# A hybrid decoder layer: four heads' values and gMLP's second half as a fourth pair of block products

## Chip, cores and metric

The kernel runs on one core of one Trainium2 chip. The metric is the device time of one execution in microseconds. A core has five engines that each work through their own list of instructions in order: TensorE (PE in the profile, with PEld for its weight loads), VectorE (DVE), ScalarE (ACT), GpSimd (POOL) and SyncE (SP), which issues most transfers. 16 DMA engines carry data between HBM and the on-chip memory SBUF; PE writes its sums into PSUM, eight banks of 128x512 float32, four of which are called acc and four dn here.

## What is computed

One layer with parallel groups of heads on 1024 tokens of width 2048, and a final RMSNorm (cut):

```
h = rmsnorm(x, ln_g)
proj = h @ w_in                       # 2048 -> 7184 columns
g_u, g_v, g_z, d_q, d_k, d_v, d_z, d_a, d_b, c_q, c_z = split(proj)
out_a = gmlp_spatial_gating(g_u, g_v, ...) * silu(g_z)      # 512 wide; layernorm(gelu(g_v)) goes in
q, k, v = split(causal_conv_silu(concat(d_q, d_k, d_v)))    # 8 heads of 128
o = gated_delta_rule(l2norm(q), l2norm(k), v, g(d_a), sigmoid(d_b))
out_b = rmsnorm(o, dn_norm_g) * silu(d_z)                   # 1024 wide
out_c = softmax(c_q mk^T) mv * silu(c_z)                    # 4 heads, 256 memory tokens
out = rmsnorm(x + concat(out_a, out_b, out_c) @ w_out, final_g)
```

The delta rule runs over the tokens in chunks: a step needs the state that the step before it left.

## The kernel before

*Numbers.* A product in float32 is made of three matmuls in a faster 32-bit format (fp32r). Each operand is split into hi, a rounded copy (ScalarE), and lo, the rest (VectorE subtracts), by split_to (416), and triple (453) adds hi hi, hi lo and lo hi in a PSUM bank. So each element that goes through PE costs a copy on ScalarE and a subtraction on VectorE first.

*Order.* No engine's order is written by hand. Every operation is recorded with a rank (a priority), and Plan (63) sorts them with prices of its own for each operation; line 274 then emits all of them, which is why nearly every row of the profile names L274. Rank 1 goes first, 9 last. together() keeps matmuls side by side, behind(op) holds back what is recorded until op is done.

*Stages.* Tokens are handled in two halves of 512 (HT), in row tiles of 128. The normalised input stands in SBUF as ahi/alo, transposed, first of half 0, then of half 1.
1. Memory's keys and values, small preparations, and the normalisation of half 0.
2. half(0) and half(1) (811): each first projects gMLP's v, tokens in rows, over 16 blocks of K into four banks (the loop at the start of half), applies gelu and a layer norm and stores it; then the decays; then for the four pairs of heads front (q and k by proj, convolution, the block matrix), values (1113: v by proj, convolution) and back (1120). proj (459) makes 128 columns for 512 tokens: 16 blocks of K, 48 matmuls of 128x512. In half(0) w_piece (433) also stores each lo part of a weight in DRAM (low), and half(1) loads it from there.
3. inverse (985) inverts the 32x32 diagonal blocks of a pair of heads on VectorE, 31 steps of two instructions over 32 partitions; levels (1014) joins them to 128x128 by small matmuls; scan_step (1061) is the recurrence, eight steps for a pair of heads and half: k times state (PE), r (VectorE), u times r (PE), ww (ScalarE), then q times state and kd times ww (PE), the new state (VectorE), ai times ww (PE), a copy (ScalarE).
4. project_pair (1274) for three pairs of 512 columns each: d_z; c_z and c_q; gMLP's z and u. Here the product of two halves of tokens, two halves of K and two halves of columns is made from seven block products in place of eight (Winograd's form of Strassen's scheme): seven (1187) makes product m from a left block (of h, or a sum of blocks, s_d) and a right block (of the weights, or a sum), each 8 blocks of K into four banks. The sums of products are made in SBUF: take1 to take7 add a bank to the tiles y.
5. out_pair (1498), twice: the same scheme for w_out on the mixed outputs, then x is added, the sums of squares taken and close (1467) scales each row tile by its root and by final_g, and sends it out, four transfers of 256 KB for each row tile and half. Products come in the order 1, 7, 6, 4, 5, 3, 2. In the second out_pair half 1 is closed at product 5 and half 0 at product 2, the last one, whose last chunks are held back so that its row tiles end one after another (last=True).

left_sums and right_sums (726, 738) make the blocks' sums, as jobs spread over stage 2; third_sum and mix_done (1327, 1364) make those of the mixed outputs on GpSimd. rights_made (1241) makes right sums of weights in SBUF; products 1 to 3 use blocks as they are, 4 to 7 sums or differences.

Of the kernel before, what the change touches and what calls it, by code (L numbers as in the profile page):

```python
# [9 lines left out]
F32 = mybir.dt.float32  # L10
# [10 lines left out]
NQ = 4  # L21
# [256 lines left out]
def kernel(  # L278
# [50 lines left out]
    class Slots:  # L329


        def __init__(self, tag, n, shape):
            self.tag, self.n, self.shape, self.i, self.made = tag, n, list(shape), 0, [None] * n

        def __call__(self, dt=F32, slot=None):
            k = self.i % self.n if slot is None else slot
# [64 lines left out]


    ident, ones, utri, mneg = (C([P, P], n) for n in ("ident", "ones", "utri", "mneg"))
# [23 lines left out]
    def split_piece(raw, eng):  # L427
        hi, lo = whi(), wlo()
        with rank(2):
            split_to(hi, lo, raw, eng)  # L430
        return hi, lo

    def w_piece(src, keep=None, first=True):

        if first:
            hi, lo = split_piece(raw_piece(src), V)
            if keep is not None:
                Q.dma_start(keep, lo.bitcast(F32))
            return hi, lo
        raw, hi, lo = raw_piece(src), whi(), wlo()  # L440
        with rank(4):
            Q.dma_start(lo.bitcast(F32), keep)
        with rank(2):
            S.copy(hi, raw)
        return hi, lo
# [3 lines left out]
    def mm(a, lhs, rhs, start, stop):  # L449
        with rank(9):  # L450
            return PE.matmul(a, lhs, rhs, start=start, stop=stop)

    def triple(a, l, r, start, stop):

        mm(a, l[0], r[0], start, False)
        mm(a, l[0], r[1], False, False)
        return mm(a, l[1], r[0], False, stop)

    def proj(w, c0, rhs, keep, first):

        a = main_bank()
        for kp in range(KT // KP):
            hi, lo = w_piece(
                w[kp * KP * P : (kp + 1) * KP * P, c0 : c0 + P].rearrange("(k p) c -> p k c", p=P), keep[kp], first
            )
            hi, lo = tok(hi), tok(lo)
            for kk in range(KP):
                k = kp * KP + kk
                triple(a, (hi[:, kk], lo[:, kk]), rhs(k), k == 0, k == KT - 1)
                if kk == 0:  # L470
                    marks.append(R.ops[-3])
        return a
# [38 lines left out]
    mrow = C([16, P], "mrow")  # L511
# [41 lines left out]
    def prep(tt, put, bank):  # L553
# [3 lines left out]
        for q in range(NQ):  # L557
            V.scalar_tensor_tensor(xq[q], xq[q], r, gb[q], op0=ALU.mult, op1=ALU.mult)
            tp = bank()
            for k in range(4):  # L560
                PE.transpose(tp[:, k * P : (k + 1) * P], xq[q][:, k * P : (k + 1) * P], ident)
            put(q, tok(tp))

# [72 lines left out]
    for h in range(NX):  # L636
# [8 lines left out]
    G.memset(mneg, 0.0)  # L645
    G.affine_select(out=mneg, in_=mneg, compare_op=ALU.is_ge, fill=NEG, base=0,
                    pattern=[[1, P]], channel_multiplier=-1)
    rows = C([96, P], "rows")
    Q.dma_start(rows, conv_w.rearrange("k (c p) -> (k c) p", p=P))
    rows2 = C([9, P], "rows2")  # L650
    Q.dma_start(rows2[0:4], gmlp_ln_g[0].rearrange("(c p) -> c p", p=P))
    Q.dma_start(rows2[4:8], gmlp_ln_b[0].rearrange("(c p) -> c p", p=P))
    Q.dma_start(rows2[8:9], dn_norm_g)
# [8 lines left out]
    PE.transpose(pt[:, 0:96], rows, ident[0:96, 0:96])  # L662
    cw = C([P, 96], "cw")
    V.tensor_scalar(cw, pt[:, 0:96], 0.5, None, op0=ALU.mult)
    pt = dnr()
    PE.transpose(pt[:, 0:9], rows2, ident[0:9, 0:9])
    col2 = C([P, 9], "col2")
    V.tensor_scalar(col2[:, 0:8], pt[:, 0:8], 0.25, None, op0=ALU.mult)
    V.tensor_scalar(col2[:, 8:9], pt[:, 8:9], 0.5, None, op0=ALU.mult)
# [41 lines left out]
    mix_d = [[DT([P, HT], f"mixd{h}_{k}") for k in range(KT)] for h in range(2)]  # L711
    hT_d = DT([KT, P, HT], "hTd")
# [3 lines left out]
    h0_d = DT([KT, P, HT], "h0d")  # L716
    o_d = [[DT([P, HT], f"od{h}_{i}") for i in range(NH)] for h in range(2)]
    v_d = [[DT([P, NT, P], f"vd{h}_{g}") for g in range(NG)] for h in range(2)]
# [4 lines left out]
    t_d = [[DT([P, HT], f"td{j}_{i}") for i in range(4)] for j in range(NH)]  # L723
    left, right = slice(0, HT), slice(HT, 2 * HT)

    def left_sums(src, dst):
        a, b, c, d = (ring["zg"]() for _ in range(4))
        with rank(6):
            for t, x_ in zip((a, b, c, d), src):
                Q.dma_start(t, x_)  # L730
            V.tensor_tensor(out=d, in0=c, in1=d, op=ALU.add)
            V.tensor_tensor(out=c, in0=a, in1=c, op=ALU.subtract)
            V.tensor_tensor(out=a, in0=d, in1=a, op=ALU.subtract)
            V.tensor_tensor(out=b, in0=b, in1=a, op=ALU.subtract)
            for t, x_ in zip((d, a, c, b), dst):
                Q.dma_start(x_, t)

    def right_sums(src, dst):
        a, b, c, d = (ring["zg"]() for _ in range(4))
        with rank(6):  # L740
            for t, x_ in zip((a, b, c, d), src):
                Q.dma_start(t, x_)
# [4 lines left out]
            for t, x_ in zip((a, d, b, c), dst):  # L747
                Q.dma_start(x_, t)

    def blk(w, k, c0):  # L750
        return w[k * P : (k + 1) * P, c0 : c0 + HT]

    def keep_h(q):
        for k in range(4 * q, 4 * q + 4):
            t = ring["zg"]()
            with rank(6):
                G.tensor_tensor(out=tok(t), in0=ahi[k], in1=alo[k], op=ALU.add)
                Q.dma_start(h0_d[k], t)

    def right_job(j):  # L760
        (c1, c2), k1, k2 = pairs[0], j, NH + j
        right_sums((blk(w_in, k1, c1), blk(w_in, k1, c2), blk(w_in, k2, c1), blk(w_in, k2, c2)), t_d[j])

    jobs = [lambda q=q: keep_h(q) for q in range(NQ)]
    jobs += [lambda j=j: right_job(j) for j in range(NH)]
    jobs += [lambda j=j: left_sums((h0_d[j], h0_d[NH + j], hT_d[j], hT_d[NH + j]), s_d[0][j]) for j in range(NH)]

    def next_job(mark=None):
        if jobs:
            with behind(mark or marks[-1]):  # L770
                jobs.pop(0)()

    def put1(tt):
        def put(q, tp):
            t = ring["tn"]()
            S.copy(t, tp.rearrange("p t c -> p (t c)"))
            Q.dma_start(hT_d[4 * q : 4 * q + 4, :, tt * P : (tt + 1) * P].rearrange("k p n -> p k n"), tok(t))

        return put

    def refill(src, k, eng):

        raw = wraw()
        Q.dma_start(raw, src[k])
        split_to(ahi[k], alo[k], tok(raw), eng)

    def wide_banks():
        i, j = turn["acc"] % 2, turn["tp"] % 2
        return [acc[1 - i], acc[3 - j], acc[i], acc[2 + j]]

    def tanh_gate(a, o):

        t = ring["tn"]()
# [4 lines left out]
    def gelu2(a, o):  # L798

        t = ring["tn"]()  # L800
# [8 lines left out]
    low_d = {}  # L809

    def half(hf):
        def project(c0):
            if hf == 0:
                low_d[c0] = [DT([P, HT], f"low{c0}_{kp}") for kp in range(KT // KP)]
            return proj(w_in, c0, ahl, low_d[c0], hf == 0)

        def to_tokens(src):
            tp = tpb()
            for tt in range(NT):
                PE.transpose(tp[:, tt * P : (tt + 1) * P], src[:, tt * P : (tt + 1) * P], ident)  # L820
            return tok(tp)


        vk = [ring[tag]() for tag in ("ai", "ai", "kd", "kd")]
        aa = wide_banks()
        for k in range(KT):
            if hf == 1:
                refill(hT_d, k, V)
            w = w_piece(w_in[k * P : (k + 1) * P, C_V : C_V + GW])
            for tt in (2, 3, 0, 1) if k == KT - 1 else range(NT):  # L830
                vmark = triple(aa[tt], (ahi[k][:, tt], alo[k][:, tt]), w, k == 0, k == KT - 1)
            if hf == 0 and k % 3 == 0 and k < 12:
                with behind(R.ops[-1]):
                    load_x(NT + k // 3, ("ut", "inv", "gt", "ut")[k // 3])
                    prep(NT + k // 3, put1(k // 3), dnr)
        for tt in (2, 3, 0, 1):
            gelu2(aa[tt], vk[tt])
        for tt in range(NT):
            s = small()
            V.bn_stats(s[:, 0:6], vk[tt])  # L840
            m = small()
            V.bn_aggr(m[:, 0:2], s[:, 0:6])
# [754 lines left out]
```

## Time and profile before

| | us |
|---|---|
| median of three runs (lowest, highest) | 1687.38 (1686.46, 1688.65) |
| the profiled execution: its own time | 1687.08 |
| its span, first to last instruction | 1685.4 |
| PE busy | 1667.4 |
| VectorE busy | 1324.0 |
| ScalarE busy | 910.1 |
| GpSimd busy | 187.3 |
| bytes moved | 401.58 MB, mean 238 GB/s |

The granted clock of PE was 0.999 over the span. A row of PE gives the duration of one matmul as its record shows it, about 0.4 us for 128x512; as matmuls are pipelined, the time between two of them is shorter, and is read from a run of them without gaps, in the chain. A 128x128 float32 matmul has two records. In a row of waits stand the waiting line, whom it waited for, the sum, how often and the longest. Names such as acc or ahi are those of the tiles, with buffer numbers left out.

### The profile page before, as it was taken

The numbers are of one execution on the slowest core, as the hardware profiler recorded it, in microseconds if no ns is written. First come the engines' busy times: TensorE is split into PE (matmuls) and PEld (weight loads), VectorE is DVE, ScalarE is ACT, GpSimd is POOL, SyncE is SP. The second block draws the span as 40 slices with busy tenths as digits, with TensorE's granted clock in tenths as the row PEclk, the third lists the DMA queues.
The fourth block names the chain that finished last, engine by engine and source line by source line (L and its number), as shares of the span: only waits on it lengthen the run. The fifth ranks groups of instructions, "written<-read, shape, count | busy, mean of one in ns | idle before, by whom it ended". The sixth has DMA issues, their size and how long they took to land.

```text
span 1685.4 us, 26930 instructions
## 1 busy us (share of the span) xinstructions
PE 1667.4 (99%) x8861; PEld 1388.9 (82%) x8861; DVE 1324.0 (79%) x2478; ACT 910.1 (54%) x2010; POOL 187.3 (11%) x163
## 2 busy tenths in 40 slices
PE   8999999999999999999999999999999999999997
PEld 7888888888888888888887888888888888888886
DVE  5856887979876576858595677889999798967797
ACT  6663654656655655656573544345653553454344
POOL 0024100100000100000000000111100121011002
PEclk9999999999999999999999999999999999999999
DMA  7798898686665868668756598877867698876577
GB/s 256 211 310 287 243 287 241 188 241 212 205 178 174 246 200 257 205 197 262 228 187 210 171 313 295 267 247 228 281 199 243 213 350 274 264 265 223 165 246 261
DMA packets 333176, 401.58 MB, mean 238 GB/s; under 512 B 50990, under 2 KB 172519, under 8 KB 333036
## 3 DMA queue, kind: packets, MB, share of 16 engines
q1 hardware_dynamic: 331300, 396.69, 73.7%
q0 software_dynamic: 1120, 2.10, 0.5%
q8 instruction: 70, 1.15, 0.3%
q10 hardware_dynamic: 616, 1.07, 0.2%
q14 instruction: 70, 0.57, 0.1%
HBM read 312.69 MB, written 87.06 MB: 237 GB/s over the span
## 4 chain that ended last, share of the span: by engine, by line
PE 97%; DVE 1%; ACT 1%; issue 1%; DMA 0%; POOL 0%; POOLq 0%; DVEq 0%; ACTq 0%
PE acc L274 75%; PE dn L274 21%; DMA kT<-in_mem_dram 0%; DVE ut L274 0%; DVE wlo L274 0%; DVE kT L274 0%; ACT jk L274 0%; DVE hs L274 0%; DVE y L274 0%; ACT whi L274 0%; ACT kT L274 0%; POOL small L274 0%; DVE tn L274 0%; DVE r L274 0%; ACT xr L274 0%
## 5 line engine op out<-in xcount | busy, mean ns | idle before, releaser
L274 PE MATMUL acc<-ahi,whi 128*128 128x512 f32 x1216 | 482.5, 397 | 0.3 <-ACT ahi L274 0.3
L274 PE MATMUL acc<-alo,whi 128*128 128x512 f32 x1216 | 482.0, 396 | 0.0
L274 PE MATMUL acc<-ahi,wlo 128*128 128x512 f32 x1216 | 481.7, 396 | 0.0
L274 ACT CAST whi<-wraw 128x512 fp32r<-128x512 f32 (+1 forms) x297 | 215.8, 727 | 240.0 <-PE acc L274 192.2
L274 PEld LDWEIGHTS acc<-ahi,wlo 128*128 128x128 f32 x1216 | 228.8, 188 | 44.3
L274 PEld LDWEIGHTS acc<-ahi,whi 128*128 128x128 f32 x1216 | 228.8, 188 | 44.3 <-ACT ahi L274 0.6
L274 PEld LDWEIGHTS acc<-alo,whi 128*128 128x128 f32 x1216 | 228.9, 188 | 43.7 <-DVE alo L274 0.4
L274 DVE TENSOR_TENSOR wlo<-wraw,whi 128x512 fp32r<-128x512 f32 (+1 forms) x201 | 183.8, 916 | 81.2 <-ACT whi L274 75.1
L274 ACT CAST ahi<-gt 128x1024 fp32r<-128x1024 f32 x75 | 78.6, 1048 | 67.0 <-DMA gt<-sd 27.9
L274 PE MATMUL acc<-whi,ahi 128*128 128x512 f32 x280 | 110.8, 396 | 0.0
L274 PE MATMUL acc<-whi,alo 128*128 128x512 f32 x280 | 110.7, 396 | 0.0
L274 PE MATMUL acc<-wlo,ahi 128*128 128x512 f32 x280 | 110.5, 395 | 0.0
L274 DVE TENSOR_TENSOR alo<-gt,ahi 128x1024 fp32r<-128x1024 f32 x75 | 94.5, 1260 | 18.7 <-ACT ahi L274 18.5
L274 PE MATMUL acc<-ahi,zh 128*128 128x512 f32 x224 | 87.9, 392 | 0.0
L274 PE MATMUL acc<-alo,zh 128*128 128x512 f32 x224 | 87.7, 392 | 0.0
L274 PE MATMUL acc<-ahi,zl 128*128 128x512 f32 x224 | 87.6, 391 | 0.0
L274 POOL TENSOR_TENSOR hs<-hs,mhalf 128x4 f32<-128x4 f32 x32 | 37.4, 1169 | 449.4 <-DVE hs L274 449.4
L274 DVE TENSOR_TENSOR alo<-inv,ahi 128x1024 fp32r<-128x1024 f32 x61 | 79.3, 1300 | 9.7 <-ACT ahi L274 9.4
L274 DVE TENSOR_TENSOR inv<-inv,y 32x31 f32<-32x31 f32 (+16 forms) x250 | 83.6, 334 | 3.7
L274 DVE TENSOR_TENSOR y<-inv,inv 32x31 f32<-32x31 f32 (+15 forms) x248 | 80.7, 325 | 3.4
L274 ACT CAST ahi<-inv 128x1024 fp32r<-128x1024 f32 x61 | 63.8, 1046 | 35.7 <-PE acc L274 10.5
L274 PEld LDWEIGHTS acc<-whi,ahi 128*128 128x128 f32 x280 | 52.7, 188 | 10.9 <-issue 0.8
(377 smaller groups left out, 3268.6 us busy)
## 6 DMA issues: line engine op xcount, KB each, us to landing
wraw<-in_w_in_dram SPq DMA_DIRECT2D x360, 256.0 KB
low<-wlo SPq DMA_DIRECT2D x96, 256.0 KB
wlo<-low SPq DMA_DIRECT2D x96, 256.0 KB
wraw<-in_w_out_dram SPq DMA_DIRECT2D x94, 256.0 KB
gt<-sd SPq DMA_DIRECT2D x84, 256.0 KB
inv<-sd SPq DMA_DIRECT2D x72, 256.0 KB
zg<-in_w_in_dram SPq DMA_DIRECT2D x32, 256.0 KB
td<-zg SPq DMA_DIRECT2D x32, 256.0 KB
```

The costliest lines, as they stand in the source:

```text
L274: o.fn(*o.args, **o.kw)
```

## The change

- **A fourth pair.** The values (v) of heads 4 to 7 and gMLP's v, 512 columns each, leave the halves and become the first of four pairs: (d_v of heads 4 to 7, g_v), (u, z), (d_z), (c_z, c_q). The pair gives gMLP's v transposed; spatial transposes it back on PE ahead of gelu and layer norm. v before the convolution goes to DRAM (p_d).
- **Late recurrences.** In each half front makes q and k of heads 4 to 7 too and stores them (late_d, gt_d). One inverse over 128 partitions inverts their blocks for both halves. values and back for these heads run with rank 2.6 beside the first later pairs.
- **Sums in PSUM.** The order of the products is 2, 1, 6, 5, 3, 7, 4; only 1, 7 and 2 start a bank, the others add to what stands in it, and ScalarE copies out what has to be kept. The differences of weights are made step by step in kept tiles, two 128x512 subtractions on VectorE for each chunk of products 1, 3, 7 and 4. All sums of mixed outputs move from GpSimd to VectorE.
- **Output.** The two output pairs are one list of 14 products, the second in the order 2 (as 12), 1, 6, 5, 3, 7, 4. Half 0 is closed at product 3, half 1 at product 4, the last. x is loaded straight into the output tiles.
- **Smaller ones.** Weights' lo parts are no longer kept in DRAM. The first projection (project_first) does the row tiles 0 to 2 of half 0 first, then tile 3: 48 matmuls of 384 columns and 48 of 128. The causal mask is set by GpSimd and the exponent by ScalarE, in place of VectorE. Both sums of a recurrence step share one bank, with q times state and ai times ww side by side.

The core of the diff:

```diff
-    pairs = ((C_DZ, C_DZ + HT), (C_CZ, C_CQ), (C_Z, C_U))
+    pairs = ((C_DV + HT, C_V), (C_U, C_Z), (C_DZ + HT, C_DZ), (C_CZ, C_CQ))
...
+    def project_first(c0):
+        a, ws = main_bank(), []
...
+        for lo, hi in ((0, NT - 1), (NT - 1, NT)):
+            for k in range(KT):
+                w = [t[:, k % KP] for t in ws[k // KP]]
+                triple(a[:, lo * P : hi * P], w, [t[:, lo:hi] for t in ahl(k)], k == 0, k == KT - 1)
+        return a
...
+        d0, d1 = scan_banks[i][:, 0:P], scan_banks[i][:, P : 2 * P]
...
+            with R.together():
+                PE.matmul(d0, q[:, sl], s, start=True, stop=False)
+                PE.matmul(d0, ai[:, tt], ww[i], start=False, stop=True)
+            PE.matmul(d1, kd[:, tt], ww[i], start=True, stop=True)
...
+    late_inv = inverse(gdrs, "late", 3)
...
+    ORDER, FIRST, SUM = (2, 1, 6, 5, 3, 7, 4), (1, 7, 2), {5: 0, 6: 1, 7: 2, 3: 3}
...
-                           i + u == 0, i + u == NH - 1)
+                           i + u == 0 and m in FIRST, i + u == NH - 1)
...
+            r = plain([blocks(*AT[m], j) for j in js])
+            parts = [(t, r[:, i * HT : (i + 1) * HT]) for i, t in enumerate(ts)]
+            if m < 4:
+                w = split_r([r])
+                if m != 2:
+                    for t, x_ in parts:
+                        minus(t, *((t, x_) if m == 1 else (x_, t)))
+                return w
+            for t, x_ in parts:
+                minus(x_, *((t, x_) if m == 7 else (x_, t)))
+            return split_r([r])
...
+        takes = {
+            2: lambda t, a: keep(yu[t], a),
+            1: lambda t, a: fin(0, 0, t, a, yu[t]),
+            6: lambda t, a: keep(yz[t], a),
+            5: lambda t, a: keep(yu[t], a),
+            3: lambda t, a: fin(0, 1, t, a),
+            7: lambda t, a: fin(1, 1, t, a, yu[t]),
+            4: lambda t, a: fin(1, 0, t, a, yz[t]),
+        }
...
+        for tt in range(NT):
+            for g in range(NG):
+                PE.transpose(hand[:, g * P : (g + 1) * P], held_v[g][:, tt * P : (tt + 1) * P], ident)
...
+    with rank(2.6):
+        for hf in range(2):
+            for p in range(NJ // 2, NJ):
+                state = front_late(p, hf, late_inv[hf * 2 + p - NJ // 2])
+                values(*state)
+                back(*state)
...
+                if (cp, m) == (1, 7):
+                    V.tensor_tensor(out=r[:, 0:1], in0=r[:, 0:1], in1=r[:, 1:2], op=ALU.add)
+                    V.tensor_tensor(out=r[:, 0:1], in0=r[:, 0:1], in1=r[:, 3:4], op=ALU.add)
+                    V.tensor_scalar(r[:, 4:5], r[:, 0:1], 1.0 / D, EPS, op0=ALU.mult, op1=ALU.add)
+                if (cp, m) in ((1, 3), (1, 4)):
+                    close(key[0], t)
...
+    seven(m_left, rights, lambda m: banks[m in (7, 4)], takes, (2, 1, 12, 6, 5, 3, 7, 4, 11, 16, 15, 13, 17, 14),
+          rows=True, last=True)
```

More of the change, by code (lines that the diff above doesn't have):

```diff
@@ L746, in right_sums, with prep1, tanh_gate @@
             V.tensor_tensor(out=c, in0=c, in1=d, op=ALU.subtract)
-            for t, x_ in zip((a, d, b, c), dst):
+            for t, x_ in zip((a, d, b, c), t_d[j]):
                 Q.dma_start(x_, t)
[L750 to L793, printed above, removed]
+    def prep1(i):
+        load_x(NT + i, "ut")
+        prep(NT + i, lambda q, tp: keep_rows(hT_d, q, i, tp), over(scan_banks))
+    def tanh_gate(a, o, ts):
+        t = ts()
         with rank(1):
@@ new lines, with refill, before @@
+    back(*state)
+    values(*ahead)
+    def refill(k):
+        raw = wraw()
+        Q.dma_start(raw, hT_d[k])
+        split_to(ahi[k], alo[k], tok(raw), V)
+    a = tpb()
+    def before(k):
+        refill(k)
+        decay_mm(a, k)
+    todo += [lambda j=j: right_sums(j) for j in range(NH)]
+    first = project([column(0, 0), column(1, 0)], before)
+    decays(1, a)
+    state = front(0, 1, first)
+    back(*ahead)
+    values(*state)
+    ahead = front(1, 1)
+    back(*state)
+    values(*ahead)
@@ L1185, in add, with seven @@
             V.tensor_tensor(out=o, in0=a, in1=b, op=ALU.add)
-    def seven(lefts, rights, banks, plan, order=range(NH), rows=False, last=False):
-        for n, (m, take) in enumerate(plan):
-            bank = banks(n)
+    ORDER, FIRST, SUM = (2, 1, 6, 5, 3, 7, 4), (1, 7, 2), {5: 0, 6: 1, 7: 2, 3: 3}
+    ends, chunk_ends = {}, [marks[-1]] * 8
+    def seven(left, right, banks, takes, order, rows=False, last=False):
+        for n, key in enumerate(order):
+            c, m = divmod(key, 10)
+            bank = banks(m) if c == 0 or m != 2 else banks(7)
             def product(t, i, a, w):
```

1139 lines of the change are left out of this document (576 added, 563 removed).

## Prediction

> **What bounds the kernel now.** I read the page's busy shares and its chain first, then TensorE's waits, then the busy time by stretches.
>
> ```profile
> span 1685.4 us, 26930 instructions
> PE 1667.4 (99%) x8861; PEld 1388.9 (82%) x8861; DVE 1324.0 (79%) x2478; ACT 910.1 (54%) x2010; POOL 187.3 (11%) x163
> ...
> PE 97%; DVE 1%; ACT 1%; issue 1%; DMA 0%; POOL 0%; POOLq 0%; DVEq 0%; ACTq 0%
> ```
>
> PE is busy 1667.4 of 1685.4 us, and the chain that ended last runs over PE for 97% of the span. So a matmul less is time less, if nothing else comes late. The second view, PE's waits, says how little comes late today:
>
> ```profile
> PE dn L274 <- DMA mrow<-in_mem_norm_g_dram: 4.3, 1, 4.3
> PE dn L274 <- DVE r L274: 1.5, 4, 0.8
> PE dn L274 <- DVE ut L274: 1.3, 3, 0.5
> PE dn L274 <- ACT ww L274: 0.5, 1, 0.5
> PE dn L274 <- ACT tblk L274: 0.5, 1, 0.5
> ```
>
> After the first load (4.3 us) some 4 us of waiting are left (1.5 + 1.3 + 0.5 + 0.5), in the recurrences and block inverses (r, ut, ww, tblk), none in the block products, as the next rows show. The third view is the busy time by stretches (length, then PE, PEld, DVE, ACT, POOL, granted clock, DMA share, GB/s):
>
> ```profile
> 300.00:350.00 50.00, 49.74 (x255) 41.59 (x254) 45.80 (x128) 35.14 (x118) 5.29 (x4) 1.00 0.67 207
> ...
> 900.00:950.00 50.00, 49.06 (x352) 40.76 (x350) 32.51 (x58) 25.13 (x58) 3.85 (x5) 1.00 0.57 180
> 1000.00:1600.00 600.00, 600.00 (x2753) 499.48 (x2752) 508.26 (x622) 286.09 (x419) 74.84 (x40) 1.00 0.76 253
> 1600.00:1676.00 76.00, 76.00 (x336) 62.70 (x334) 68.49 (x105) 35.92 (x57) 11.42 (x11) 1.00 0.73 249
> 1676.00:1685.40 9.40, 0.07 (x1) 0.00 (x0) 3.05 (x6) 3.28 (x6) 0.65 (x2) 0.73 0.79 295
> ```
>
> Two things matter below. In the block products (1000 to 1600) PE never rests, but VectorE is busy 508 of 600 us, 85%, and 90% in the last 76: it is the second limit. And the last 9.4 us hold no matmul; they are output alone.
>
> **The change, part by part.** *Matmuls.* The price of one 128x512 product comes from the chain:
>
> ```profile
> 951.60 184.76 PE acc L274 x815
> ...
> 1371.43 21.76 PE dn L274 x96
> ```
>
> 184.76 / 815 = 0.2267 us, and 21.76 / 96 the same. Removed: the values of heads 4 to 7, 4 heads x 2 halves x 16 blocks of K x 3 = 384 matmuls, and gMLP's v, 2 halves x 16 x 4 row tiles x 3 = 384; together 768. Added: seven products for these 1024 columns, each 8 blocks of half of K x 3 x 4 banks = 96, so 672. Net -96, or **-21.8 us**.
>
> The first projection is now cut in two (384 columns, then 128), so 48 matmuls become 96. No row shows a 384-column one; the nearest are:
>
> ```profile
> L274 PE MATMUL acc<-alo,whi 128*128 128x512 f32 x1216 | 482.0, 396 | 0.0
> ...
> L274 PE MATMUL acc<-inv,whi 128*128 128x256 f32 x64 | 18.2, 289 | 0.0
> ...
> L274 PE MATMUL dn<-ww,kd 128*128 128x128 f32 x128 | 24.7, 275 | 0.5 <-ACT ww L274 0.5
> ...
> L274 PE MATMUL acc<-ident,qT 128*128 128x128 f32 x64 | 9.7, 272 | 0.0
> ```
>
> 256 columns less shorten one by 396 - 289 = 107 ns, 0.42 ns a column. That makes 384 columns 0.227 - 0.054 = 0.173 us and 128 columns 0.066; from above, a 128x128 record is busy 24.7 / 128 = 0.19 and a 384-column one can't exceed 0.227. Taking 0.173 and 0.09 (the slope is nearer, since these are the same kind of matmul): 48 x 0.263 = 12.6 for the 48 x 0.227 = 10.9 before, **+1.7** (bounds +0.6 to +9). The layer norm needs v with tokens in partitions, and the pair gives it transposed: 2 halves x 4 x 4 = 32 transposes of 128x128, at 9.7 / 64 = 0.15 us, **+4.8** (0 where they fall into idle time, up to 32 x 0.272 = 8.7). The rest of PE's list is the same in number. PE's sum: -21.8 + 1.7 + 4.8 = **-15.3**.
>
> The Trainium skill prices these otherwise ("TensorE: Matmul & The Clock Gate", section "Back-to-back issue gap"): warm, columns / 2.4 + 2.5 ns. By it the cut pair is 48 x (0.1625 + 0.0558) = 10.5 us, an estimate, and the term would be -0.4 where I take +1.7; for 512 columns it gives 0.216 where the trace has 0.2267.
>
> *The tail.* This term speaks against the change. Before, the last two products of the output (numbers 3 and 2) use weight blocks as loaded, and VectorE closes tiles 0 to 2 of the last half beside them; what is left behind PE is little:
>
> ```profile
> 1669.00:1672.00 3.00, 3.00 (x15) 2.50 (x14) 2.09 (x7) 2.04 (x5) 0.55 (x1) 1.00 0.09 33
> ...
> 1675.00:1678.00 3.00, 1.07 (x5) 0.56 (x3) 2.04 (x5) 2.15 (x6) 0.55 (x1) 1.00 1.00 370
> 1678.00:1680.00 2.00, 0.00 (x0) 0.00 (x0) 1.22 (x3) 1.15 (x3) 0.55 (x1) 1.00 1.02 376
> 1680.00:1682.00 2.00, 0.00 (x0) 0.00 (x0) 0.09 (x1) 0.27 (x1) 0.00 (x0) 0.59 1.02 379
> 1682.00:1684.00 2.00, 0.00 (x0) 0.00 (x0) 0.00 (x0) 0.00 (x0) 0.00 (x0) 0.50 0.71 264
> ```
>
> The issues and single steps of the closing, from the timeline (start, us, engine):
>
> ```profile
> 1671.06 0.33 SPq L274 DMA_DIRECT2D out_dram<-kT  x1
> ...
> 1675.75 4.83 SPq L274 DMA_DIRECT2D out_dram<-y  x5
> ...
> 1680.30 0.34 ACTq L274 DMA_DIRECT2D out_dram<-qT  x1
> ...
> 1676.11 0.69 DVE L274 TENSOR_TENSOR y<-acc,y 128x512 f32<-128x512 f32 x1 [0.63 <-PE acc L274]
> ...
> 1678.36 0.55 POOL L274 TENSOR_TENSOR small<-small,mhalf 128x1 f32<-128x1 f32 x1 [2.25 <-DVE small L274]
> ...
> 1678.94 0.72 ACT L274 ACTIVATE kT<-kT,small 128x512 f32<-128x512 f32 x1 [0.85 <-POOL small L274]
> ```
>
> PE ends at 1676.1. Nine output transfers of 262,144 bytes are issued after that (five by SyncE, four by ScalarE), they fill the DMA engines at 370 to 379 GB/s, and the span ends 9.3 us after PE. In the changed kernel the last two products (7 and 4) take their right blocks as differences: 2 products x 4 chunks x 2 = 16 more 128x512 subtractions on VectorE, some 0.69 us each as the add above, 11 us in a stretch where it was busy 90%, so that at most 76.00 - 68.49 = 7.5 us were free in all 76. VectorE's order shows the effect: it first finishes the 16 scalings of half 0, then the sums of squares of all four row tiles of half 1, and each tile's last step stands behind the add of the last tile, which waits for PE's last matmul. So all 16 transfers of half 1 (4.19 MB) come behind PE's end. Add (0.69), a small step, GpSimd's root (0.55) and the first scaling (0.72), with the hand-overs, put the first issue at 2.8 us; transfers start some 1.2 later (an issue at 1671.06, and only 9% of DMA time used up to 1672); 4.19 MB at 376 GB/s take 11.2; from the last byte to the span's end it was 2 (71% of the two us from 1682, so 1683.4, to 1685.4). That is 17 us, **+7.8** over 9.3 (bounds: +4 if the queues start at once and the end costs less, +10 if VectorE's scalings pace them).
>
> *Sums in PSUM, kept weight tiles, spare copies.* Sums of the products now run on in the banks, which takes adds from VectorE and gives copies to ScalarE; the bank copies stand beside three other banks' work (24 x 0.2267 = 5.4 us a bank), so they cost nothing unless ScalarE, 48% busy there (286.09 of 600), is late. The 96 stores and 96 reloads of split weights go; SyncE and DMA were not on the chain (0%), so nothing is gained. Third sums move from GpSimd to VectorE: hidden, but they add to VectorE's 85%.
>
> *Recurrences.* Heads 4 to 7 now run beside products of pairs 0 and 1, and their inverses as one over 128 partitions:
>
> ```profile
> L274 DVE TENSOR_TENSOR wlo<-wraw,whi 128x512 fp32r<-128x512 f32 x128 | 90.0, 706 | 43.7 <-ACT whi L274 39.4 <-ACT ww L274 1.8 <-PE dn L274 1.3
> ...
> L274 DVE TENSOR_TENSOR alo<-gt,ahi 128x1024 fp32r<-128x1024 f32 x75 | 94.5, 1260 | 18.7 <-ACT ahi L274 18.5
> ...
> L274 DVE TENSOR_TENSOR inv<-inv,y 32x31 f32<-32x31 f32 (+16 forms) x250 | 83.6, 334 | 3.7
> L274 DVE TENSOR_TENSOR y<-inv,inv 32x31 f32<-32x31 f32 (+15 forms) x248 | 80.7, 325 | 3.4
> ```
>
> An inverse step costs 0.33 us whether over 32 or 128 partitions as far as the elements in a row set it, so five inversions in place of eight free VectorE of about 3 x 62 x 0.33 = 61 us, off the path. But each step of a recurrence makes PE wait for r, ww and the new state, and queued behind the waiting matmul is every later product. In VectorE's new order there are about twice as many places as before where 1 to 5 us of work (in one, 16 inverse instructions, 16 x 0.33 = 5.3 us) stand ahead of what PE needs next. Before, such places cost 4 us. I take **+2**: bounds 0, if PE's stock covers them, and +12, if all the added work shows.
>
> **Sum.** The profiled execution took 1687.08 us (1685.4 span and 1.7 around it), 0.3 below the median of the three runs. 1687.1 - 15.3 + 7.8 + 2 = 1681.6; with the 0.3 the median would be 1681.9. I call it **1681.5**.
>
> **Rivals.**
> *A, only the matmuls count*: the outputs get out beside PE after all, and no stall is added. 1687.4 - 15.3 = 1672. For it: PE is 97% of the chain. Against: VectorE's order and its 90%.
> *B, VectorE becomes the wait of the late recurrences; slower.* 4 heads x 2 halves x 4 tiles = 32 steps with three waits each, 96, now share VectorE with splits of 1.26 us, where the steps of before mostly met splits of 0.71. If one wait in five meets such a split, 19 x 1.26 = 24 us: 1681.5 - 2 + 24 = 1703. It decides from 1690.8 - 1679.5 = 11.3 us, 0.12 us per wait. For it: 85% busy, longer instructions. Against: the steps of before cost 4 us over 64 steps though VectorE was busy 45.80 of 50 us beside some (300 to 350).
> *C, the same in part*: 5 to 11 us of such stalls; the time stays at 1684 to 1690.8, no change.
> *D, one long idle time brings the clock down.* The rows from 1678 to 1682 show full clock for about 4 us after the last matmul and 0.5 afterwards; a stall that long in mid-kernel would be followed by matmuls at half clock. The place with 16 inverse instructions is the only candidate: 4 us more of waiting and then 4 us at half clock, of which 2 are lost: 1681.5 - 2 + 6 = 1685.5. The Trainium skill says it too ("TensorE: Matmul & The Clock Gate", section "HAM oscillation — how this bites in real kernels"): an idle gap above about 3.4 us brings the half clock back. By its figure the same place would lose 1.7 us, an estimate; the trace's end agrees with the rule, with about 4 us in place of 3.4.
>
> **How the numbers follow.** Forecast (1677 to 1684) 0.50; A (below 1677) 0.14; C 0.16; D 0.05; B (above 1690.8) 0.15. A difference of 0.2%, 3.4 us, is about what a measurement of this kernel can tell from no change. Faster by more than that (below 1684.0): forecast and A, 0.64. Within: C and D, 0.21. Slower: B, 0.15. Range: 1670 (A, with the cut projection free) to 1691 (C's end); outside lie most of B and little else.
>
> **What would show it.** PE's busy time about 15 us lower, at the same 0.2267 us per product; from PE's last matmul to the end about 17 us, with 16 output transfers behind it; PE's waits on r, st and ww of 4 to 8 us in sum, with the longest under 4. The forecast is wrong if the waits reach 11 us, if the pace of the products changes, if the granted clock falls below 1.00 between 50 and 1650 us, or if half of the outputs leave before PE's end.

## The result and the profile after

| | before | changed |
|---|---|---|
| median, us | 1688.02 (4 executions, 1686.46 to 1688.81) | 1700.06 (4, 1696.01 to 1704.49) |
| the profiled execution: its own time | 1687.08 | 1704.49 |
| its span | 1685.4 | 1702.8 |

The changed kernel is slower: ratio 1.0073, 95% interval 1.0046 to 1.0100, some 12 us. Its executions lie 8.5 us apart, those of before 2.4, and the profiled one is the slowest of its four; a share of what follows is larger in it than in the median. The page of the changed kernel, the lines that answer to those of before:

```profile
span 1702.8 us, 26597 instructions
PE 1663.3 (98%) x8844; PEld 1377.5 (81%) x8844; DVE 1317.4 (77%) x2351; ACT 980.6 (58%) x2166; POOL 120.8 (7%) x125
...
PE 84%; DMA 6%; DVE 5%; ACT 2%; issue 1%; SPq 1%; POOL 0%; ACTq 0%; DVEq 0%; POOLq 0%
```

PE is busy only 4 us less than before (1667.4), where the count promised 15, and the chain that ended last runs over PE for 84% of the span, not 97: DMA has 6% and VectorE 5%. The waits of PE (sum, times, longest), the first eight rows:

```profile
PE dn L274 <- DMA rows<-in_mem_norm_g_dram: 4.3, 1, 4.3
PE dn L274 <- DVE st L274: 3.6, 8, 1.1
PE dn L274 <- ACT tblk L274: 3.2, 3, 2.1
PE dn L274 <- DVE ut L274: 2.0, 1, 2.0
PE dn L274 <- DVE inv L274: 1.7, 1, 1.7
PE dn L274 <- ACT ww L274: 1.3, 1, 1.3
PE dn L274 <- ACT vs L274: 1.1, 2, 0.7
PE acc L274 <- ACT ahi L274: 1.0, 1, 1.0
```

Before, all after the first load came to 4 us; here many names share some 18. The stretches of the changed kernel (length, PE, PEld, DVE, ACT, POOL, granted clock, DMA share, GB/s):

```profile
50.00:200.00 150.00, 146.81 (x791) 124.12 (x790) 107.53 (x220) 99.59 (x276) 15.45 (x26) 0.99 0.72 210
200.00:340.00 140.00, 137.43 (x647) 113.70 (x646) 118.27 (x246) 87.61 (x256) 16.39 (x11) 1.00 0.71 216
340.00:410.00 70.00, 66.86 (x433) 54.33 (x432) 59.03 (x170) 40.68 (x114) 6.15 (x4) 0.95 0.50 143
410.00:610.00 200.00, 196.62 (x1192) 162.43 (x1191) 163.09 (x392) 133.39 (x404) 24.01 (x21) 1.00 0.61 179
610.00:700.00 90.00, 86.66 (x534) 71.56 (x533) 52.51 (x101) 57.66 (x151) 7.33 (x9) 1.00 0.74 232
700.00:1050.00 350.00, 346.92 (x2111) 286.49 (x2110) 266.97 (x462) 210.72 (x421) 20.83 (x22) 1.00 0.74 240
1050.00:1660.00 610.00, 610.00 (x2779) 506.88 (x2778) 490.29 (x668) 298.26 (x450) 16.42 (x12) 1.00 0.74 247
1686.40:1702.80 16.40, 0.01 (x1) 0.00 (x0) 5.47 (x13) 5.73 (x10) 2.63 (x4) 0.62 0.72 261
```

From 1050 us PE runs without a pause; the idle time lies ahead of it, in the halves (up to 610), at the change to the pairs (610 to 700) and beside the late recurrences (700 to 1050). The last row is the tail: 16.4 us, 9.3 before.

To compare kernels I use **lost time**: from the trace's records of PE, the time from each matmul's start to the next one's, less a price for its kind, summed. The prices are set by the trace of before (0.2269 us for 512 columns, 0.126 for 256, 0.118 for a record of a 128x128 float32 product, 0.120 for one of a transpose, 0.023 and 0.085 for the 32 and 64 wide, about 0.7 for the ten of a single row), with 0.171 and 0.075 for the new 384 and 128 columns. Lost time holds idle time, lost clock and broken pipelining alike, and any error of a price: the 128-column matmuls took 0.111 us each, so 48 x 0.036 = 1.7 us of it stands where they run (50 to 200 us). In us:

```
stretch        0-50  50-200 200-340 340-410 410-610 610-700 700-1050 1050-end  sum
before          3.4   -0.3    -0.1     0.6    -0.2     0.0      2.2     -0.7    4.9
changed         3.3    7.6     2.9     7.3     4.4     3.8      4.0     -0.9   32.4
```

At those prices PE's list is worth 1666.5 us before and 1649.3 after: **-17.2**. Lost time **+27.5**, tail **+7.1**; the sum, +17.4, is the difference of the two spans (1702.8 - 1685.4).

### The profile page after: what moved, and what is told of

Its sections match the earlier page's. It is cut to its first block, busy times and chain, and to the rows that moved or that the text cites. A ratio compares the mean times of both kernels' runs of the same rounds, so it can differ in the third digit from the quotient of the medians.

```text
span 1702.8 us, 26597 instructions
## 1 busy us (share of the span) xinstructions
PE 1663.3 (98%) x8844; PEld 1377.5 (81%) x8844; DVE 1317.4 (77%) x2351; ACT 980.6 (58%) x2166; POOL 120.8 (7%) x125
## 4 chain that ended last, share of the span: by engine, by line
PE 84%; DMA 6%; DVE 5%; ACT 2%; issue 1%; SPq 1%; POOL 0%; ACTq 0%; DVEq 0%; POOLq 0%
PE acc L274 68%; PE dn L274 16%; DVE wlo L274 1%; DMA sd<-zg 1%; DMA wraw<-in_w_in_dram 1%; DVE inv L274 1%; SPq L274 1%; ACT whi L274 1%; DVE ai L274 1%; DMA E<-gcd 0%; DMA ut<-in_x_dram 0%; DMA zg<-in_w_in_dram 0%; DVE tn L274 0%; DVE kT L274 0%; DVE zg L274 0%
## 5 line engine op out<-in xcount | busy, mean ns | idle before, releaser
L274 PE MATMUL acc<-ahi,whi 128*128 128x512 f32 (+2 forms) x1256 | 496.1, 396 | 1.9 <-ACT ahi L274 1.0
L274 PE MATMUL acc<-alo,whi 128*128 128x512 f32 (+2 forms) x1256 | 496.2, 395 | 0.0
L274 PE MATMUL acc<-ahi,wlo 128*128 128x512 f32 (+2 forms) x1256 | 496.1, 395 | 0.0
L274 PE MATMUL acc<-ahi,zh 128*128 128x512 f32 x592 | 187.2, 394 | 0.0
L274 ACT CAST ahi<-y 128x1024 fp32r<-128x1024 f32 x112 | 117.7, 1051 | 77.6 <-PE acc L274 46.3
L274 PEld LDWEIGHTS acc<-ahi,zh 128*128 128x128 f32 x592 | 110.0, 188 | 21.4
L274 DVE TENSOR_TENSOR alo<-y,ahi 128x1024 fp32r<-128x1024 f32 x56 | 68.6, 1226 | 26.5 <-ACT ahi L274 26.4
L274 DVE TENSOR_TENSOR alo<-raws,ahi 128x1024 fp32r<-128x1024 f32 x56 | 68.3, 1220 | 22.8 <-ACT ahi L274 22.6
L274 DVE TENSOR_TENSOR ahi<-y,ahi 128x1024 fp32r<-128x1024 f32 x56 | 68.8, 1228 | 13.0 <-ACT ahi L274 12.8
L274 PE MATMUL acc<-zh,ahi 128*128 128x512 f32 x192 | 61.4, 390 | 0.0
```

The source lines that it names most:

```text
L274: o.fn(*o.args, **o.kw)
```

## The experiments

All times are medians; the kernel before lies at 1687.5 to 1689.5 beside each. "Lost" is lost time of the profiled execution. Expectations are the text on record.

**1. The block sums on GpSimd.**

```diff
 def left_sums(j): / def right_sums(j):
-            V.tensor_tensor(out=d, in0=c, in1=d, op=ALU.add)
+            G.tensor_tensor(out=d, in0=c, in1=d, op=ALU.add)
... (the eight other sums and differences of the two functions likewise)
```

> Two theories of the 27 us that PE loses beside its counted work in the changed kernel. Q (blocked queues): an instruction at the head of VectorE's or ScalarE's in-order queue waits for a transfer that lands later than the order assumes, and what PE needs stands behind it; the block sums made beside the halves are the worst case (their tiles cost VectorE 16.1 us of waiting for transfers, 3.1 before). L (late steps): the recurrences of heads 4 to 7 wait behind VectorE's long instructions beside the pairs. Here the block sums of left and right blocks are made by GpSimd, so that their waits leave VectorE. Q: PE's lost time between 200 and 500 us falls by 4 to 8 us, and the time by as much, to 1692 to 1696 us. L: no change, 1700 within 3 us.

Measured: 1747.40 us, lost 75.3. VectorE's waits on the sums' tiles are gone, but GpSimd's own groups (count, busy, mean ns, idle before) and one stretch say what came in their place:

```profile
L274 POOL TENSOR_TENSOR zg<-zg,zg 128x512 f32<-128x512 f32 x40 | 57.8, 1445 | 20.8 <-DMA sd<-zg 15.7 <-DMA zg<-in_w_in_dram 3.3
...
L274 POOL TENSOR_TENSOR zg<-zg 128x512 f32<-128x512 f32 x24 | 35.8, 1492 | 79.5 <-DMA zg<-in_w_in_dram 66.1 <-DMA zg<-hTd 13.0
...
485.00:490.00 5.00, 0.80 (x2) 0.50 (x2) 2.77 (x2) 1.14 (x2) 4.44 (x4) 0.50 0.75 244
```

A sum takes 1.45 us, twice VectorE's, and GpSimd stands 100.3 us before these two groups (20.8 + 79.5), 98.1 of it for transfers (15.7 + 3.3 + 66.1 + 13.0). GpSimd also makes the roots that q and k wait for, and they stand behind. PE is idle for 4 of these 5 us, and its clock stands at half from 481.6 to 519.1 us. Neither theory forecast this. It says that an engine's queue blocked by transfers does cost PE, and that GpSimd is a worse place for it; it doesn't tell Q from L.

**2. No late recurrences.**

```diff
-                state = front_late(p, hf, late_inv[hf * 2 + p - NJ // 2])
-                values(*state)
-                back(*state)
+                for h in (2 * p, 2 * p + 1):
+                    t = ring["vs"]()
+                    Q.dma_start(t, late_d[hf][h - NJ][0])
+                    Q.dma_start(o_d[hf][h], t)
```

> Leaves out the late recurrences of heads 4 to 7 (their levels, steps and norms; another array of the right shape is stored in their place). By the counts PE has 63.6 us less to do (160 and 64 products of 128x128, 64 of 64x64, 160 of 32x32). L: beside that nearly all the lost time goes, some 20 us more: 1616. Q: only what is lost after 640 us can go, 4 to 8 us: 1628 to 1632, and the losses before 640 us (about 24 us of 32) stay.

Measured: 1636.89 us, 63.2 below the changed kernel with 63.6 less to do. Lost 29.0; from 700 to 1050 us -0.5 (4.0), up to 610 still 24.3 (25.5). PE has no pause from 700 to 1000:

```profile
700.00:1000.00 300.00, 300.00 (x1368) 249.17 (x1367) 239.08 (x339) 150.14 (x190) 7.27 (x10) 1.00 0.79 251
```

L falls: the late recurrences lose 4 us or so. Q's time, 1628 to 1632, isn't reached either. The price of the prediction's rival B was near the result, but not its place.

**3. A lighter closing of half 0.**

```diff
+                if (cp, m) == (0, 3):
+                    for b in range(2):
+                        G.tensor_tensor(out=y[0, b][t], in0=y[0, b][t], in1=fg[b], op=ALU.mult)
...
-            if half_ == 0 or c == 2:
+            if c == 2 or (half_ == 0 and c == 3):
                 V.scalar_tensor_tensor(y, y, r[:, 5:6], fg[c], op0=ALU.mult, op1=ALU.mult)
```

> Tail alone: half 0's first two column blocks are multiplied by final_g on GpSimd during the first output pair, and its closing scales them on ScalarE, so that VectorE has eight 128x512 scalings less in the last two products, and in its order the tiles of half 1 close one after another during the last product. If VectorE's backlog makes the tail, the time from PE's end to the span's end falls from 16.4 to 9 to 11 us and the time by 5 to 7, to 1693 to 1695. If the 16 transfers themselves set it, under 2 us.

Measured: tail 10.3 us (16.4), as forecast; PE ends at 1682.3. In the changed kernel PE ends at 1686.4, and the first and last of SyncE's twelve issues of half 1 are

```profile
1688.65 0.33 SPq L274 DMA_DIRECT2D out_dram<-inv  x1
...
1697.37 1.15 SPq L274 DMA_DIRECT2D out_dram<-gt  x1
```

here the first of them leaves 4 us ahead of PE's end, and the last one comes 4.5 behind it:

```profile
1678.00 0.33 SPq L274 DMA_DIRECT2D out_dram<-y  x1
...
1686.87 0.78 SPq L274 DMA_DIRECT2D out_dram<-gt  x1
```

The time is 1698.52 (1694.32 to 1699.03), only 1.5 lower. The place is shown; how much of it reaches the median of this kernel can't be read from five executions that lie 5 us apart, and lost time (28.7) moved within such a spread.

**4 and 5. More time for transfers in the plan**, everywhere, and only for what the halves record.

```diff
-    DMA_FIXED = 1600.0
+    DMA_FIXED = 4000.0
```

> The planner is told that a transfer takes 4.0 us, not 1.6, from its issue to its landing beside its bytes (in the trace 4 to 8 us in the chain); nothing else is changed, the work is the same. Q: instructions that wait for transfers are put later in the queues of VectorE and ScalarE, their waits for transfers fall by half, and the time falls by 8 to 14 us, to 1686 to 1692. L: no change within 3 us. If the order was already late enough, PE gets transfers later and it is slower.

```diff
+            o.lat += self.room
```

> As the run with 4.0 us for transfers, but only for what is recorded up to the late inverse; the pairs keep 1.6. With 4.0 us everywhere PE's lost time before 600 us fell from 22 to 9 us and after 600 us rose from 9 to 18. Q (instructions that wait for transfers stand too early in the queues of VectorE and ScalarE): both halves of that separate, so lost time is 9 before 600 and 9 after, and the time falls by 8 to 13 us, to 1687 to 1692. If the losses after 600 us come from the later start of the halves' own work, they stay at 18 and the time stays at 1698 to 1702.

`room` is 2400 ns up to the late inverse and 0 from there on. Measured: 1701.05 and 1699.58: nothing. VectorE's waits for transfers did shrink. The rows of VectorE's waits on DMA sum to 16.4 us before, 52.6 in the changed kernel and 21.8 with 4.0 us; its first and third to fifth rows in the changed kernel:

```profile
DVE wraw L274 <- DMA wraw<-in_w_in_dram: 10.6, 10, 1.7
...
DVE zg L274 <- DMA sd<-zg: 7.8, 5, 2.5
DVE zg L274 <- DMA zg<-in_w_in_dram: 6.7, 3, 5.4
DVE kd L274 <- DMA wraw<-in_w_in_dram: 5.1, 3, 2.3
```

and with 4.0 us everywhere the two largest:

```profile
DVE zg L274 <- DMA zg<-in_w_in_dram: 7.4, 2, 4.6
DVE y L274 <- DMA el<-od: 4.0, 1, 4.0
```

Lost time up to 610 us fell from 25.5 to 14.0, and from 610 on rose from 6.9 to 14.6 (with room in the halves alone: 16.3 and 12.8). So the waits that Q names are real, and Q is wrong in that taking them away pays: lost time came back elsewhere.

**6. The first projection cut in two equal parts.**

```diff
-        for lo, hi in ((0, NT - 1), (NT - 1, NT)):
+        for lo, hi in ((0, NT // 2), (NT // 2, NT)):
```

> The first projection is cut after row tile 1, not 2: 96 matmuls of 256 columns in place of 48 of 384 and 48 of 128. In the changed kernel the 128-column ones follow each other by 0.110 us (0.173 for 384), and the granted clock drops to 0.66 from 85 to 90 us without an idle time ahead of it. Theory H (a stretch of half-filled matmuls takes the clock down): here no such stretch is left, the clock stays at 1.00 between 75 and 100 us, and PE's lost time there falls from 3.8 to about 1; with the counted work (96 x 0.126 for 13.6 us, -1.5) the time falls by 2 to 4 us. Rival: the clock drops because of the wait for row tile 3 around 68 to 79 us; then it drops here too and nothing is gained.

Measured: 1697.20 (1693.53 to 1698.15), 2.9 lower, with executions that overlap those of the changed kernel; lost from 50 to 200 us 3.6 (7.6). Of these 4.0 us 1.7 are the price of the 128-column matmuls and 1.7 the clock. Clock in the changed kernel, by the microsecond, and then here:

```profile
80.00:85.00 5.00, 5.00 (x38) 4.17 (x37) 2.55 (x5) 1.55 (x3) 0.00 (x0) 1.00 0.56 189
85.00:86.00 1.00, 1.00 (x11) 1.00 (x11) 0.55 (x1) 0.62 (x1) 0.00 (x0) 1.00 0.57 127
86.00:87.00 1.00, 1.00 (x7) 1.00 (x7) 0.69 (x1) 0.00 (x1) 0.00 (x0) 0.51 1.14 341
87.00:88.00 1.00, 1.00 (x4) 0.86 (x4) 0.23 (x1) 0.88 (x2) 0.00 (x0) 0.50 0.37 103
```

```profile
80.00:85.00 5.00, 5.00 (x28) 3.71 (x27) 2.76 (x6) 2.68 (x6) 0.00 (x0) 1.00 0.96 269
85.00:90.00 5.00, 5.00 (x27) 4.13 (x25) 2.90 (x7) 0.20 (x1) 0.00 (x0) 1.00 0.90 243
```

In the changed kernel PE works from 80.1 to 86.9 through the 48 matmuls of 128 columns, one weight load after the other (11 loads fill 1.00 us), and from 83.7 to 84.8 through two products of a single row; it has no pause, and at 86.0 the clock halves for 3.4 us. With 256 columns around the same two products it stays at 1.00, as it does in the kernel before, where they stand among 512 columns. H is right in part. Of the kernels here nine have the 48, and in six of them (the changed kernel, 1, 2, 3, 5 and 9) the clock fell beside these two products. It stayed at 1.00 in 4, 7 and 8, though in 8 the two stand among the 48 (at 83.5 to 84.6 us, the 48 from 78.3 to 85.0):

```profile
80.00:90.00 10.00, 10.00 (x59) 8.21 (x59) 6.65 (x10) 4.43 (x10) 0.00 (x0) 1.00 0.64 186
```

The trace's own record of the clock, each change with its time, shows an order in this. Within a trace the drops lie whole multiples of 3.413 us apart (those of the changed kernel at 86.0 and 359.1 by 80 of them), and half clock in mid-kernel lasts 3.4 us or a multiple, up to 37.5 in experiment 1. In all six, the 3.4 us of this grid that end at the drop hold both single-row products, and beside them at most 0.4 us that isn't a 128-column matmul. In 4, 7 and 8 the 3.4 us with the two products hold 1.0 us of other work; 3.4 us of 128-column matmuls alone (in 3, 4 and 7) brought nothing down. That fits all nine kernels, but no edit tested it.

**7. More room for PE in the plan, and a control.**

```diff
-    SLACK = 600.0
+    SLACK = 1500.0
```

> The planner puts an instruction of PE 1.5 us, not 0.6, behind the planned end of what it needs on other engines; the work is the same. Theory T (tight places): PE's losses are many small waits because the changed order leaves PE little stock between the steps of a chain; with 1.5 us the waits halve, lost time falls from 32 to 15 to 20 us, and the time by 8 to 14, to 1686 to 1692. Theory P (few large places: the first projection, the half's change, the pair's change, each waiting on transfers and full queues): lost time falls by under 5 us.

> Control: the kernel before with 1.5 us of room for PE. Its lost time is 4.9 us in all, 0.6 after the first load and what the pace makes up; the time should stay within 2 us of 1687.5 if its order has stock enough, and rise by several us if more room makes the chains of the halves run out of cover.

Measured: 1723.68 in the changed kernel (lost 50.5), 1696.01 in the kernel before (14.3, of it 11.0 between 200 and 340 us). T falls, and P doesn't forecast 24 us more either. So falls the idea that the order before has stock to spare: it lost 9 us more by this one number.

**8. Room, transfers and tail together.** Edits 3, 4 and 7.

> Three edits together: 1.5 us of room for PE, 4.0 us for transfers, and the lighter closing of half 0 (tail of 10 us in place of 16). If the terms add up as T has them, 16.4 - 10.3 = 6 us come from the tail and 10 to 15 from the waits: 1680 to 1686, equal to the kernel before or a little faster. If waits only move from one place to another (as with the 4.0 us alone): 1692 to 1696, the tail's gain alone.

Measured: 1712.14, lost 42.0, tail 12.0, above both expectations. Terms don't add up.

**9. Free raw tiles for pair 0.** The wait at the pair change, in the chain of experiment 6's execution (start, us) and in its stretches:

```profile
639.49 4.79 DMA raws<-in_w_in_dram
...
651.08 0.94 ACT ahi L274
...
650.00:660.00 10.00, 7.90 (x23) 5.84 (x24) 6.95 (x20) 7.20 (x24) 1.42 (x2) 0.66 0.95 327
```

The load is issued behind the last projection (638.2), whose tile it takes; the split of it comes at 651, PE waits 2.6 us and then runs at half clock.

```diff
-    raws = halves(heir(alq[1], "raws", "alo1"))
+    raws = [heir(b, f"raws{i}", f"zg{i}", 2 * HT) for i, b in enumerate(zgb)]
+    zhl = halves(heir(alq[1], "zhl", "alo1", dt=F32R))
...
-    wraw2 = over([*kvraw[:2], raws[1]])
+    wraw2 = over([raws[1], *kvraw[:2]])
```

> The raw tiles of the first left and right chunk of pair 0 are taken from the four tiles of the block sums' jobs, free from 480 us on, in place of a tile of the half's input, which is free only behind the last projection; the third hi and lo tiles go there instead. In the changed kernel the loads are issued behind the last projection's last matmul, land 4.8 us later, and PE waits (0.31 + 0.99 in the profiled execution, 2.6 in another, with the clock at 0.66 for 10 us). If that wait is the pair change's loss, lost time between 600 and 700 us falls from 4 to 6 to 1 to 2, and the time by 3 to 5 us, to 1695 to 1697. If the chain on ScalarE sets it (q and k of the last head), under 1 us.

Measured: lost from 610 to 700 us 1.7 (3.8); the time 1701.12 (1694.84 to 1709.70). The place answers, the median doesn't show it.

**10 and 11. Three edits (3, 6, 9), and with room for transfers in the halves (5).**

> Three edits that each answer to one place: lighter closing of half 0 (tail), the first projection cut into 256 and 256 columns (clock), the free raw tiles (pair change). If places add up: -6, -3, -4 on 1700, so 1687; if the gain of one is eaten at the next place: 1692 to 1695.

> The three edits and the room for transfers in the halves. If all of it adds up: 1687 - 10 = 1677, below the kernel before, which would leave 4 us of the count's gain (17) unfound. If the room only moves waits: as the three edits alone.

Measured: 1688.64 with three (11 executions, 1684.25 to 1691.73; ratio to before 1.0000, interval 0.9991 to 1.0010): 11.4 below the changed kernel and level with the one before. Its span of 1687.0 stands 1.6 over before's 1685.4, and that adds up: the list's worth -16.9, lost time 22.3 in place of 4.9 (+17.4), tail 10.3 in place of 9.3 (+1.0). With four 1688.05 (0.9991, 0.9980 to 1.0001), lost 22.1: no more. The three gain together what each alone hardly showed. How much of the 11.4 is the three places and how much is that this is another order, the runs don't separate.

**12. Cover given back.** On the three edits:

```diff
-                    triple(a, (hi[:, kk], lo[:, kk]), ahl(k), k == 0, k == KT - 1)
+                    triple(a, (hi[:, kk], lo[:, kk]), ahl(k), k == 0, False)
+                    mm(a, lo[:, kk], ahl(k)[1], False, k == KT - 1)
```

> The kernel of three edits, and each projection of the halves but the first makes a fourth matmul for each block of K, the product of the two lo parts: 624 matmuls more, 141.5 us by the count, with no load, split or copy more. That gives the halves back most of the PE time that the change took from them (174 us). Theory C (cover lost): the work of VectorE, ScalarE and the transfers in the halves stayed while PE's shrank, so chains that PE's work hid now show. Then lost time falls from 22 to 8 to 12 us, and the time is 1688.6 + 141.5 - 12 = 1818. Theory P (fixed places of the new order): 19 to 24 us stay lost, 1828 to 1832.

Measured: 1833.67, lost 23.6. C falls: 141.5 us more of PE work, each matmul with a weight load of its own on PE and hardly anything else, took no lost time away.

**13 and 14. Less room, and two banks for a step.** On the three edits: SLACK = 200.0; and

```diff
+        if h < NJ:
+            d0, d1 = dnr.bufs[2 * i][:, 0:P], dnr.bufs[2 * i + 1][:, 0:P]
```

> The kernel of three edits with 0.2 us of room for PE in the plan, not 0.6 (1.5 made the changed kernel 24 us and the one before 8 us slower). C: chains are the limit in the halves, a plan that delays them less gains up to 5 us: 1684 to 1688. If 0.6 stands at the point where waits and room balance: 1688 to 1693.

> The kernel of three edits with the two sums of a recurrence step of heads 0 to 3 in banks of their own, as before the change, not in one. If the shared bank lengthens the steps (a copy out of the one sum holds back the other), lost time between 225 and 600 us falls from 10 to 5 us and the time by 3 to 5; else nothing changes within 2 us, or it rises because the small products of the inverses find fewer banks free.

Measured: 1701.76 (lost 36.7), above both expectations, and 1692.93 (26.4; from 200 to 610 us, where the halves' steps run, 10.3 in place of 10.9). The shared bank isn't the cause.

**15, 16 and 17. Other numbers for the kernel before; a middle one for the changed.** DMA_FIXED = 4000.0 and SLACK = 200.0 in the kernel before; edit 11 with 1000 for 2400.

> Control: the kernel before with 4.0 us for transfers in the plan. Theory F (the order before is a fitted one): PE's 4.9 us of lost time there belong to one order that the planner's numbers give for one list of work; any other number gives an order that loses 10 to 30 us, as 1.5 us of room for PE did (14.3), so 1693 to 1705. Theory N (the changed list is harder to order): the kernel before takes the change of numbers within 4 us.

> Control: the kernel before with 0.2 us of room for PE. The kernel of three edits lost 14 us more with it. F: as much here, 1697 to 1705. N: within 4 us of 1688.

> The three edits with 1.0 us more for transfers in the halves (0 gave 1688.6, 2.4 gave 1688.1). F: another order, lost time anywhere from 15 to 30 us, 1682 to 1697, with no trend between 0 and 2.4. If the transfers' room mattered by itself it would lie at 1688 with both.

Measured: 1731.38 (lost 46.9), 1694.60 (12.7) and 1688.12 (0.9995, 0.9986 to 1.0004; lost 19.9). The kernel before with 4.0 us for transfers loses most where it was safest, in the output's products:

```profile
1050.00:1550.00 500.00, 498.35 (x2303) 414.85 (x2302) 426.49 (x527) 240.08 (x365) 82.81 (x40) 1.00 0.78 255
1550.00:1610.00 60.00, 46.65 (x173) 35.93 (x172) 35.30 (x41) 18.83 (x25) 0.00 (x0) 0.90 0.49 157
```

For the kernel before F has the direction: each of three other numbers cost it time, 5 to 42 us against the kernel before beside it. It has not the sizes (1693 to 1705 forecast where 1731.38 came, 1697 to 1705 where 1694.60 came), and the 1688.12 of the middle number fits both of its theories. N isn't dead: the changed list lost 19.9 us or more in each of the fourteen orders tried with the work of the kernel whole, before's 4.9 to 46.9 in four.

## Why the prediction was wrong

1. *What bounds the kernel* (PE, with VectorE second): right.
2. *Matmuls* (-15.3): right; at the prices above the list fell by 17.2, and by 15.5 with the 128-column ones at the 0.111 us that they took (0.09 in the prediction). The 384-column ones follow each other by 0.173 us as worked out, a transpose's records by 0.11 to 0.12 (0.15 taken). What the cut also cost, and the term left out, was the clock (point 5).
3. *The tail* (+7.8): right, +7.1, by the mechanism named: VectorE's order puts all of half 1 behind the last matmul, first issue 2.25 us after it (2.8 forecast), and eight scalings less on VectorE (experiment 3) bring the tail to 10.3.
4. **The step that failed is the sum's only term for waits, "Recurrences. ... Before, such places cost 4 us. I take +2: bounds 0 ... and +12".** Where it looked it was right: beside the late recurrences lost time rose from 2.2 to 4.0 us (experiment 2 makes it some 4), and PE's waits on r, st and ww came to 5.3 us (0.4 + 3.6 + 1.3; 4 to 8 forecast). But it put the rest of the new order at nothing, without a reason. Lost time rose by 27.5 us in the profiled execution, and about 23 in a median one (1700.06, 4.4 lower): 7.9 from 50 to 200 us, over half of it around the first projection (65 to 95), 6.7 at the change of halves (340 to 410), 3.8 around the change to the pairs (610 to 700), 7.6 in the halves beside these. I read the 4 us of waiting in the trace of before as what such a kernel loses, and scaled it. It belongs to one order: three other numbers in the plan make the kernel before lose 13 to 47 us (experiments 7, 15, 16). The stock that hides a wait isn't visible in a trace in which it is hidden. Of the signs of being wrong that the prediction named, the clock below 1.00 in mid-kernel came. The waits on r, st and ww did not reach its 11 us, because the added waits stand elsewhere: PE's waits after the first load come to 18 us in all.
5. *Rivals.* B gave 1703 with a chance of 0.15; its size was near, its mechanism wrong. D's clock came true at two places in the profiled execution, 1.7 us at 86 and some 3.4 at 359 to 366:

```profile
352.55 2.65 DMA wraw<-hTd
...
355.87 0.36 ACT ut L274
...
359.00:362.00 3.00, 3.00 (x20) 2.21 (x18) 2.44 (x7) 1.58 (x3) 0.00 (x0) 0.52 0.63 163
362.00:365.00 3.00, 3.00 (x10) 2.38 (x9) 1.60 (x5) 1.10 (x2) 0.00 (x0) 0.50 0.72 218
```

   A reload of half 1's input lands at 355.2, ScalarE has stood before it, and the copies that the block inverse needs (ut, tblk) stand behind; PE waits 2.1 us (354.9 to 357.0), makes sixteen 64-wide products and some of 512 columns, and stands at half clock from 359.1 to 365.9. The 16 inverse instructions that D named were not the place. The Trainium skill ("TensorE: Matmul & The Clock Gate", section "HAM oscillation — how this bites in real kernels") asks for an idle gap of 3.4 us; here 2.1 us with thin work behind it did, and at 86 us no gap at all.
6. *What stays open.* Three places are found (tail, first projection, pair change), and the kernel without them is 11.4 us faster. Some 17 us of added lost time remain in it and eat the 17 us of fewer matmuls: some twenty waits of 0.2 to 1.7 us after the first load, 13 to 14 us in sum where before has 4, and the rest as a slower pace without a pause. They aren't lost cover (12), one bank for a step (14) or the late steps (2), and another planned time of transfers or room for PE alone doesn't take them away (4, 5, 7, 13). That the planner's numbers suit the old list better is likely after 7, 15 and 16, but no numbers were found that suit the new one, so it is argued and not shown.

## What to carry to other kernels

Where the order of the work is planned, the idle time in the trace of before is a property of that order, not of the kernel: an edit that makes a new order should be priced with the idle time that other orders of the same work show. Runs with a changed planner constant measure that: three of them gave 13, 14 and 47 us here, so one alone says little of the size. Read the end of each engine's queue for what stands behind the last matmul; that forecast held to a microsecond. When several places lose a few microseconds each in a kernel whose executions spread as much, test them together as well as one by one.

## What the runs showed of the hardware

- The granted clock halved with PE busy throughout: after 5.9 us of 128-column matmuls 0.111 us apart (11 weight loads fill 1.00 us) with 1.1 us of single-row products among them it stood at 0.50 from 86.0 to 89.4 us. With 256 columns around the same products it stayed at 1.00, and with 128 columns it fell in six kernels of nine.
- Drops of the clock within a trace lay whole multiples of 3.413 us apart, and half clock in mid-kernel lasted 3.4 us or a multiple (3.4 and 6.8 in the changed kernel, 37.5 in experiment 1).
- A wait of 2.1 us with sixteen 64-wide products behind it was followed by 6.8 us at half clock, so this wait cost 5 to 6 us, not 2.
- GpSimd's 128x512 addition took 1.45 to 1.6 us where VectorE's took 0.68.
